# Four expert tiles instead of three with each routing head, the index lookup on VectorE alone, and three tiles ahead of the slots' transposes

## The chip, the cores and the metric

The kernel runs on one core of one Trainium2 chip. The metric is the device time of one execution in microseconds (us), as the median of several executions. TensorE is called PE below (its weight loads PEld), VectorE DVE, ScalarE ACT, GpSimd POOL and SyncE SP; L53 is line 53 of the kernel before.

## What is computed

Two layers of a streaming encoder on 512 tokens of 1024 channels, in float32: a convolution with gated linear attention, then an attention with forget gates. Each layer ends with a PEER feed-forward part, and only that part is touched by the change. Cut to what matters:

```python
PEER_HEADS = 8; PEER_NKEYS = 128; PEER_TOPK = 16        # 128*128 experts, 128 slots per token

def peer_ffn(h, wq, keys, u, v):
    q = (h @ wq).reshape(B, S, PEER_HEADS, 2, half)
    s1 = einsum('bshd,hnd->bshn', q[..., 0, :], keys[:, 0])
    s2 = einsum('bshd,hnd->bshn', q[..., 1, :], keys[:, 1])
    v1, i1 = top_k(s1, 16);  v2, i2 = top_k(s2, 16)
    cand = (v1[..., :, None] + v2[..., None, :]).reshape(B, S, PEER_HEADS, 256)
    sc, j = top_k(cand, 16)
    experts = take_along_axis(i1, j // 16) * 128 + take_along_axis(i2, j % 16)
    gates = softmax(sc)
    act = gelu(einsum('td,ted->te', h, u[experts]))
    return einsum('te,ted->td', gates * act, v[experts])
```

## The kernel before

A PEER part (`peer`, `peer_body`; once for each layer) runs in three stretches.

**Routing.** The loop over 8 heads projects the queries of a head (`proj_T` twice: 24 matmuls of 512 columns each), multiplies them with the keys (L990), copies the scores to SBUF (`sd`, L991) and calls `route`. That does, on DVE, the top 16 of each of the two key halves for four token blocks (`topk`, L740 to L745), the 64 candidate sums, and their top 16. The lookup of the indices is a closure, `lookup()`, that runs a head later: ACT casts the indices (`ix`, L773), DVE takes the differences of neighbouring ones (`dx`, L777), ACT spreads each difference over 16 places (`st`, L780), DVE compares positions with steps (`oh`, L798, twice), multiplies by the spread differences (L801) and folds the products (L805, L807) into the ids `E`. All these are bf16.

**Expert tiles.** With 128 tokens the experts' rows are gathered by indirect DMA; for the other 352 tokens all 16384 experts are computed densely, 128 at a time: 128 tiles of the matrix u. A tile (`u_step`) loads 512 KB, splits the float32 weights into a high part (ACT, `whi`, L52) and a low part (DVE, or POOL where the call says so, `wlo`, L53), and makes 24 matmuls of 352 columns into the PSUM tile `pu`; ACT takes the Gelu (`xact` or `act`, L871). `WQU` = 3 tiles are written behind each head's `route`, so 24 belong to the routing. 32 of the first tokens of the second block are gathered as well (`x_u`: a gather on POOL, then a dot product of 1024 elements on DVE, L897); up to `XR` = 2 such rows go with each head.

**The rest of the first half.** After the last head, the gates are normalised (`gates`, L820 on), PE transposes the ids and gates of the slots (`flip`, L929), and 104 more tiles follow. With them go 96 pieces of `gate4` (POOL, ACT and DVE make one-hot tiles `a1`, `a2`, PE multiplies them, L959, ACT copies the result to `big`) at an even pace from the first tile on to `TAIL` = 8 tiles before the end, and the gathers that are left with their dots (L881).

**The second half** sweeps 128 tiles of the matrix v (L1053) and gathers rows of v (L914).

The order on each engine is not the program's. The scheduler of the framework orders the instructions of the whole program by its own simulated times, and each engine then takes its row first in, first out. `issue_after` pins an instruction behind another. So the counts below are taken from the order on each engine.

## Time and profile before

| | us |
|---|---|
| median of 3 runs (lowest, highest) | 3182.42 (3172.59, 3187.05) |
| the profiled execution's own time | 3180.49 |
| its span, first to last instruction | 3178.7 |
| layer 0, first scores of the routing to the transposes | 304.7 to 540.0 |
| layer 0, transposes to the end of the first half | 540.0 to 1031 |
| layer 1, the same two stretches | 1918.0 to 2147.8 to 2640 |

The share of busy time is read by stretch: an engine that is busy for nearly all of a stretch, and that the others wait for, bounds it. In rows of the timeline the brackets hold the idle time of that engine just before the instruction and what ended it. PEclk is the clock that was granted to TensorE, as a share of 2.4 GHz.

### The profile page before, as it was taken

Reading aid. Unit: us, or ns where it says so; the run is one execution under the profiler, and the core shown is the slowest. Engines: PE = TensorE matmul, PEld = TensorE weight load, DVE = VectorE, ACT = ScalarE, POOL = GpSimd, SP = SyncE. Lnnn points to the kernel's source line nnn. Section 1 sums busy time; section 2 is a strip of 40 time slices with the busy share of each in tenths; the row PEclk is TensorE's granted clock in tenths of the full one; section 3 lists DMA queues with packets and bytes.
Section 4 is the critical chain, followed back from the end, with each engine's and each line's share of the span. In section 5 each row is a group of like instructions: output and inputs, shape, how many; then the busy total and the mean of one; then the engine's idle time right before and its main releaser. Section 6 shows DMA issues by size and latency. Waiting matters only on the chain.

```text
span 3178.7 us, 46471 instructions
## 1 busy us (share of the span) xinstructions
PE 3024.8 (95%) x15934; PEld 2635.8 (83%) x15934; DVE 2466.8 (78%) x5338; ACT 1541.1 (48%) x2668; POOL 1394.1 (44%) x1072
## 2 busy tenths in 40 slices
PE   8999996999999999999999989969999999999999
PEld 6767886999999888887766669869999997887787
DVE  7764999888787888888546538998877888888886
ACT  4353334777765333333356624337667753333333
POOL 1321233999786233333100012328999983332330
PEclk9999997999999999999999999989999999999999
DMA  4104554999999999999421125558999999999996
GB/s 154 60 27 131 178 182 137 344 368 357 338 336 337 323 355 359 346 358 346 149 80 43 39 83 178 166 181 293 340 347 330 342 340 332 369 354 336 361 346 211
DMA packets 343808, 815.00 MB, mean 256 GB/s; under 512 B 27897, under 2 KB 182922, under 8 KB 337426
## 3 DMA queue, kind: packets, MB, share of 16 engines
q1 hardware_dynamic: 260626, 510.00, 46.2%
q0 software_dynamic: 82944, 302.03, 26.8%
q8 instruction: 125, 2.05, 0.3%
q14 instruction: 113, 0.93, 0.1%
HBM read 717.74 MB, written 93.06 MB: 255 GB/s over the span
## 4 chain that ended last, share of the span: by engine, by line
PE 74%; DVE 8%; DMA 2%; ACT 1%; issue 1%; POOL 0%; SPq 0%; DVEq 0%; ACTq 0%; POOLq 0%
PE acc L1053 32%; PE pu L75 9%; PE pu L77 9%; PE pu L76 9%; PE bank L959 5%; PE bank L77 2%; PE bank L75 2%; PE bank L76 2%; PE po L672 1%; PE bank L640 1%; DVE wlo L53 1%; DVE gr L897 1%; DVE tk L743 1%; DMA raw<-in_vF_dram 1%; ACT whi L52 1%
## 5 line engine op out<-in xcount | busy, mean ns | idle before, releaser
L52 ACT ACTIVATE whi<-raw 128x1024 fp32r<-128x1024 f32 x604 | 634.7, 1056 | 643.2 <-PE pu L76 310.6
L53 DVE TENSOR_TENSOR wlo<-raw,whi 128x1024 fp32r<-128x1024 f32 x565 | 693.0, 1227 | 194.8 <-ACT whi L52 193.8
L75 PE MATMUL pu<-hhi,whi 128*128 128x352 f32 x2048 | 687.1, 335 | 13.3 <-ACT xact L871 10.2
L77 PE MATMUL pu<-hhi,wlo 128*128 128x352 f32 x2048 | 671.8, 328 | 12.9 <-DVE wlo L53 11.9
L76 PE MATMUL pu<-hlo,whi 128*128 128x352 f32 x2048 | 669.3, 327 | 0.6 <-DVE hlo L115 0.6
L914 POOL DMA_INDIRECT gr<-in_vF_dram,ids x256 | 329.6, 1287 | 664.0 <-DVE x L916 620.2
L1053 PE MATMUL acc<-wlo,wh 128*128 128x512 f32 x1536 | 474.4, 390 | 0.0
L1053 PE MATMUL acc<-whi,wl 128*128 128x512 f32 x1536 | 471.7, 389 | 0.0
L1053 PE MATMUL acc<-whi,wh 128*128 128x512 f32 x1536 | 430.7, 392 | 24.1 <-ACT wh L52 13.8
L52 ACT ACTIVATE wh<-gc 128x384 fp32r<-128x384 f32 x256 | 134.2, 525 | 644.5 <-PE acc L1053 628.0
L879 POOL DMA_INDIRECT gr<-in_uN_dram,ids x256 | 406.3, 1587 | 83.3 <-issue 37.1
L942 POOL TENSOR_SCALAR a<-cst,sT 128x128 f32<-128x128 f32 x384 | 425.7, 1118 | 38.2 <-ACT sT L930 19.3
L75 PEld LDWEIGHTS pu<-hhi,whi 128*128 128x128 f32 x2048 | 391.6, 191 | 17.8 <-ACT xact L871 12.7
L77 PEld LDWEIGHTS pu<-hhi,wlo 128*128 128x128 f32 x2048 | 390.5, 191 | 14.4 <-DVE wlo L53 13.1
L76 PEld LDWEIGHTS pu<-hlo,whi 128*128 128x128 f32 x2048 | 391.5, 191 | 1.7 <-DVE hlo L115 0.9
L1053 PEld LDWEIGHTS acc<-whi,wh 128*128 128x128 f32 x1536 | 288.7, 189 | 88.4 <-ACT whi L52 14.6
L1053 PEld LDWEIGHTS acc<-wlo,wh 128*128 128x128 f32 x1536 | 289.8, 189 | 60.3
L1053 PEld LDWEIGHTS acc<-whi,wl 128*128 128x128 f32 x1536 | 288.6, 188 | 59.9
L916 DVE SCALAR_TENSOR_TENSOR x<-gr,dots,x 128x1024 f32<-128x1024 f32 x256 | 327.4, 1279 | 0.4
L881 DVE CUSTOM_DVE_ANT_0 gr<-gr,h 128x1024 f32<-128x1024 f32 x256 | 309.5, 1230 | 15.7 <-DMA gr<-in_uN_dram,ids 14.9
L53 POOL TENSOR_TENSOR wlo<-raw,whi 128x1024 fp32r<-128x1024 f32 x39 | 101.4, 2606 | 497.6 <-ACT whi L52 497.5
L53 DVE TENSOR_TENSOR wl<-gc,wh 128x384 fp32r<-128x384 f32 x256 | 141.9, 555 | 120.9 <-ACT wh L52 118.5
(264 smaller groups left out, 4529.4 us busy)
## 6 DMA issues: line engine op xcount, KB each, us to landing
raw<-in_uT_dram SPq DMA_DIRECT2D x256, 512.0 KB
raw<-in_vF_dram SPq DMA_DIRECT2D x256, 512.0 KB
G<-big SPq DMA_DIRECT2D x48, 1024.0 KB
gc<-G SPq DMA_DIRECT2D x32, 1536.0 KB
aside<-xact SPq DMA_DIRECT2D x208, 176.0 KB
at<-aside SPq DMA_DIRECT2D x104, 352.0 KB
raw<-in_w_in_dram SPq DMA_DIRECT2D x32, 512.0 KB
raw<-in_wq_dram SPq DMA_DIRECT2D x32, 512.0 KB
```

The costliest lines, as they stand in the source:

```text
L52: first = self.nc.scalar.activation(hi, raw, AF.Copy)
L53: self.last_lo = (eng or self.nc.vector).tensor_tensor(lo, raw, hi.bitcast(F32), op=ALU.subtract)
L75: mm(out, lh, rh, start=first, stop=False)
L76: mm(out, lh, rl, start=False, stop=False)
L77: return mm(out, ll, rh, start=False, stop=last)
L879: nc.gpsimd.indirect_dma_start(out=r, out_offset=None, in_=uN, in_offset=bass.IndirectOffsetOnAxis(ap=ids[:, s:s + 1], axis=0))
L881: return lambda: nc.vector.tensor_tensor_reduce(r, r, h0, 1.0, 0.0, ALU.mult, ALU.add, accum_out=dots[:, s:s + 1])
L914: nc.gpsimd.indirect_dma_start(out=r, out_offset=None, in_=vF, in_offset=bass.IndirectOffsetOnAxis(ap=ids[:, s:s + 1], axis=0))
L916: return lambda: nc.vector.scalar_tensor_tensor(self.x0, r, dots[:, s:s + 1], self.x0, op0=ALU.mult, op1=ALU.add)
L942: nc.gpsimd.tensor_scalar(a2[:, t], self.iota, e2[:, t:t + 1], None, op0=ALU.is_equal)
L959: nc.tensor.matmul(p[:, t], a2[:, t], a1[:, t], start=True, stop=True)
L1053: nc.tensor.matmul(acc[b][c], wt[:, s], vt[:, c], start=(n == 0 and wt is wh and vt is vh), stop=(n == NE1 - 1 and wt is wl))
```

## The change

It does four things. `WQU` is 4, so 32 tiles are written with the heads and 96 behind them. The lookup is no longer a closure that runs a head later: it stands at the end of `route`, all of it on DVE, without the copies `ix` and `st` (the differences come from the integer indices, and the multiplication reads `dx` with each element repeated 16 times). `PLAIN` = 3 tiles stand ahead of the transposes and of the first piece of `gate4`; the 96 pieces are paced over the 85 tiles from there to `TAIL`. `XR` is 3 for every head.

```diff
@@ -30,7 +30,7 @@
 TX = 32
 XQ = P // TX
 TU = TD - TX
-XR = 2
+XR = 3
 TG = 16
 NTG = TD // TG
 EC = 8
@@ -38,7 +38,8 @@
 ROWS = 5
 LAG = 2
 AHEAD = 4
-WQU = 3
+WQU = 4
+PLAIN = 3
 TAIL = 8
 NEG = -3.0e38
 TILE = {"schedule_with_timeline_sim": True}
@@ -766,48 +767,39 @@
         for b in range(n):
             self.topk(sb, cand[:, b], 64, SC[:, b, hd], j[:, b])
 
-        def lookup():
-
-            ix = sb.tile([P, n, 2, 1 + TOPK], BF16, name="ix")
-            nc.gpsimd.memset(ix[:, :, :, 0:1], 0.0)
-            nc.scalar.activation(ix[:, :, :, 1:], i1, AF.Copy)
-            dx = sb.tile([P, 2, n, TOPK], BF16, name="dx")
-            ixw = ix.rearrange("p b w k -> p w b k")
-            for w in range(2):
-                nc.vector.tensor_tensor(dx[:, w], ixw[:, w, :, 1:], ixw[:, w, :, 0:TOPK], op=ALU.subtract)
-            wide = [P, 2 * n, TOPK, TOPK]
-            st = sb.tile([P, 2 * n, TOPK * TOPK], BF16, name="st", tag="rs", bufs=2)
-            nc.scalar.activation(st.rearrange("p b (r k) -> p b r k", k=TOPK),
-                                 dx.rearrange("p w b r -> p (w b) r")[:, :, :, None].to_broadcast(wide), AF.Copy)
-            jf = sb.tile([P, n, TOPK], F32, name="jf")
-            nc.vector.tensor_copy(jf, j)
-
-
-            pl = sb.tile([P, 2, n, TOPK], BF16, name="pl")
-            nc.scalar.activation(pl[:, 0], jf, AF.Copy)
-            bits = sb.tile([P, 3, n, TOPK], U32, name="bits")
-            j2 = sb.tile([P, 3, n, TOPK], F32, name="j2")
-            for k, (m, end) in enumerate(((3, 56.0), (4, 40.0), (8, 16.0))):
-                nc.vector.tensor_scalar(bits[:, k], j, m, None, op0=ALU.bitwise_and)
-                nc.vector.scalar_tensor_tensor(j2[:, k], jf, end, bits[:, k], op0=ALU.is_lt, op1=ALU.mult)
-            nc.vector.tensor_tensor(j2[:, 0], j2[:, 0], j2[:, 1], op=ALU.add)
-            nc.vector.tensor_tensor(pl[:, 1], j2[:, 0], j2[:, 2], op=ALU.add)
-
-            oh = sb.tile([P, 2 * n, TOPK * TOPK], BF16, name="oh", tag="rs", bufs=2)
-            for w in range(2):
-                nc.vector.tensor_tensor(oh[:, w * n:(w + 1) * n].rearrange("p b (r k) -> p b r k", k=TOPK),
-                                        pl[:, w, :, None, :].to_broadcast([P, n, TOPK, TOPK]),
-                                        self.steps[:, w, None].to_broadcast([P, n, TOPK, TOPK]), op=ALU.is_ge)
-            nc.vector.tensor_tensor(oh, oh, st, op=ALU.mult)
-
-            for m in (1, 2, 4):
-                pair = oh.rearrange("p b (r h m) -> p b r h m", h=2, m=m * TOPK)
-                nc.vector.tensor_tensor(pair[:, :, :, 0, 0:TOPK], pair[:, :, :, 0, 0:TOPK], pair[:, :, :, 1, 0:TOPK],
-                                        op=ALU.add)
-            nc.vector.tensor_tensor(E[:, :, :, hd].rearrange("p w b k -> p (w b) k"), oh[:, :, 0:TOPK],
-                                    oh[:, :, 8 * TOPK:9 * TOPK], op=ALU.add)
-
-        return lookup
+        dx = sb.tile([P, 2, n, TOPK], BF16, name="dx")
+        ixw = i1.rearrange("p b w k -> p w b k")
+        nc.vector.tensor_copy(dx[:, :, :, 0:1], ixw[:, :, :, 0:1])
+        nc.vector.tensor_tensor(dx[:, :, :, 1:], ixw[:, :, :, 1:], ixw[:, :, :, 0:TOPK - 1], op=ALU.subtract)
+
+
+        jf = sb.tile([P, n, TOPK], F32, name="jf")
+        nc.vector.tensor_copy(jf, j)
+        pl = sb.tile([P, 2, n, TOPK], BF16, name="pl")
+        nc.vector.tensor_copy(pl[:, 0], jf)
+        bits = sb.tile([P, 3, n, TOPK], U32, name="bits")
+        j2 = sb.tile([P, 3, n, TOPK], F32, name="j2")
+        for k, (m, end) in enumerate(((3, 56.0), (4, 40.0), (8, 16.0))):
+            nc.vector.tensor_scalar(bits[:, k], j, m, None, op0=ALU.bitwise_and)
+            nc.vector.scalar_tensor_tensor(j2[:, k], jf, end, bits[:, k], op0=ALU.is_lt, op1=ALU.mult)
+        nc.vector.tensor_tensor(j2[:, 0], j2[:, 0], j2[:, 1], op=ALU.add)
+        nc.vector.tensor_tensor(pl[:, 1], j2[:, 0], j2[:, 2], op=ALU.add)
+
+        oh = sb.tile([P, 2 * n, TOPK * TOPK], BF16, name="oh")
+        for w in range(2):
+            nc.vector.tensor_tensor(oh[:, w * n:(w + 1) * n].rearrange("p b (r k) -> p b r k", k=TOPK),
+                                    pl[:, w, :, None, :].to_broadcast([P, n, TOPK, TOPK]),
+                                    self.steps[:, w, None].to_broadcast([P, n, TOPK, TOPK]), op=ALU.is_ge)
+        ohs = oh.rearrange("p b (r k) -> p b r k", k=TOPK)
+        nc.vector.tensor_tensor(ohs, ohs, dx.rearrange("p w b r -> p (w b) r")[:, :, :, None].to_broadcast(
+            [P, 2 * n, TOPK, TOPK]), op=ALU.mult)
+
+        for m in (1, 2, 4):
+            pair = oh.rearrange("p b (r h m) -> p b r h m", h=2, m=m * TOPK)
+            nc.vector.tensor_tensor(pair[:, :, :, 0, 0:TOPK], pair[:, :, :, 0, 0:TOPK], pair[:, :, :, 1, 0:TOPK],
+                                    op=ALU.add)
+        nc.vector.tensor_tensor(E[:, :, :, hd].rearrange("p w b k -> p (w b) k"), oh[:, :, 0:TOPK],
+                                oh[:, :, 8 * TOPK:9 * TOPK], op=ALU.add)
 
     def gates(self, sb, SC):
 
@@ -965,14 +957,7 @@
 
 
         nu = 0
-        xq, rows, lookups = [], [], []
-
-        def found():
-            f, hd = lookups.pop(0)
-            f()
-            x_ids(hd)
-            xq.extend((x_u, (hd, c)) for c in range(XQ))
-
+        xq, rows = [], []
         with tc.tile_pool(name=f"pr{L}", bufs=2, reuse_waits="tile") as rb:
             for hd in range(HEADS):
                 qT = []
@@ -989,18 +974,16 @@
                     for w in range(2):
                         nc.tensor.matmul(p[:, w], qT[w][:, b * P:(b + 1) * P], kt[:, w], start=True, stop=True)
                     nc.scalar.activation(sd[:, b], p.rearrange("p a b -> p (a b)"), AF.Copy)
-                lookups.append((self.route(rb, sd, E, S, hd), hd))
+                self.route(rb, sd, E, S, hd)
+                x_ids(hd)
+                xq.extend((x_u, (hd, c)) for c in range(XQ))
                 for i in range(WQU):
                     lo, mm = u_step(nu, nc.gpsimd if nu < 2 or nu > 12 and nu % 2 else None)
                     nu += 1
-                    if i == 0 and hd:
-                        with tc.issue_after(lo.ins):
-                            found()
                 with tc.issue_after(lo.ins):
                     for f in rows:
                         f()
-                rows = pump(xq, XR if hd < HEADS - 1 else 2 * XR)
-            found()
+                rows = pump(xq, XR)
             self.gates(rb, S)
         nc.vector.tensor_scalar(idf, E[:, 0, 0].rearrange("p h k -> p (h k)"), float(NE1),
                                 float(L * NE1 * P), op0=ALU.mult, op1=ALU.add)
@@ -1008,14 +991,12 @@
 
 
         with tc.tile_pool(name=f"pu{L}", bufs=2, reuse_waits="tile") as ub:
-            for b in range(nd):
-                flip(b)
             groups = [(b, tg) for b in range(nd) for tg in range(P // TG)]
             groups = groups[TX // TG:] + groups[0:TX // TG]
             gates = [(gate4, (ub, b, tg, g)) for b, tg in groups for g in range(TG // 4)]
             gathers = xq + [(g_u, (s,)) for s in range(SLOTS)]
             nx = len(xq)
-            ng, nq = len(gates) / (NE1 - TAIL - nu), len(gathers) / (NE1 - LAG - nu)
+            ng, nq = len(gates) / (NE1 - TAIL - PLAIN - nu), len(gathers) / (NE1 - LAG - nu)
             cg = cq = 0.0
             products, rows = [], [rows] + [[] for _ in range(LAG - 1)]
             while nu < NE1:
@@ -1024,9 +1005,13 @@
                 with tc.issue_after(mm.ins):
                     for f in products:
                         f()
-                cg += ng
-                products = pump(gates, cg)
-                cg -= int(cg)
+                    if nu == HEADS * WQU + PLAIN:
+                        for b in range(nd):
+                            flip(b)
+                if nu >= HEADS * WQU + PLAIN:
+                    cg += ng
+                    products = pump(gates, cg)
+                    cg -= int(cg)
                 with tc.issue_after(lo.ins):
                     for f in rows.pop(0):
                         f()
```

Behind the last head of layer 0, ACT prepares the tiles (`whi`), takes their Gelu (`xact`) and makes the lookup's copies, up to the first copy of transposed slots (`sT`). Before:

```order
L871 ACTIVATE xact<-pu 128x352
L52 ACTIVATE whi<-raw 128x1024
L871 ACTIVATE xact<-pu 128x352
L52 ACTIVATE whi<-raw 128x1024
L773 ACTIVATE ix<-i_4292 128x8x16
L52 ACTIVATE whi<-raw 128x1024
L780 ACTIVATE st<-dx 128x2048
L787 ACTIVATE pl<-jf 128x64
L820 ACT_TABLE_LOAD
L820 ACTIVATE S<-S 128x512
L930 ACTIVATE sT_2054<-bank 128x384
```

Now:

```order
L863 ACTIVATE xact<-pu 128x352
L53 ACTIVATE whi<-raw 128x1024
L863 ACTIVATE xact<-pu 128x352
L53 ACTIVATE whi<-raw 128x1024
L863 ACTIVATE xact<-pu 128x352
L53 ACTIVATE whi<-raw 128x1024
L812 ACT_TABLE_LOAD
L812 ACTIVATE S<-S 128x512
L53 ACTIVATE whi<-raw 128x1024
L922 ACTIVATE sT_2054<-bank 128x384
```

The copies `ix`, `st` and `pl` are gone from ACT. On PE the tiles counted in each order before a layer's first transpose are 27 before and 37 now, in both layers; 101 and 91 follow it.

On DVE, the lookup of a middle head of layer 0 (`oh`, `dx`, `pl`), among the top-k of the next head and splits of tiles (`wlo`). Before:

```order
L794 TENSOR_TENSOR pl<-j_3491 128x64
L743 MATCH_REPLACE tk<-v_3364,sd 128x128 x2
L798 TENSOR_TENSOR oh<-pl,steps 128x1024
L744 MAX v_3364<-tk 128x8 x2
L53 TENSOR_TENSOR wlo<-raw,whi 128x1024
L801 TENSOR_TENSOR oh<-oh,st 128x2048
L745 MAX_INDEX i_3365<-v_3364,tk 128x8 x2
L805 TENSOR_TENSOR oh<-oh 128x64x16
```

Now:

```order
L779 CAST pl<-jf 128x64
L784 SCALAR_TENSOR_TENSOR j_3621<-jf,bits 128x64 x3
L790 TENSOR_TENSOR oh<-pl,steps 128x1024
L785 TENSOR_TENSOR j_3621<-j_3621 128x64
L786 TENSOR_TENSOR pl<-j_3621 128x64
L790 TENSOR_TENSOR oh<-pl,steps 128x1024
L741 MAX v_3874<-sd 128x8 x2
L794 TENSOR_TENSOR oh<-oh,dx 128x2048
```

One cast came over from ACT, and the multiplication takes `dx` in place of `st`. Counted from the first scores to the last write of `E` in a layer, DVE now makes 28 dots (L897) instead of 21, and 32 splits (L53) in layer 0 and 33 in layer 1 instead of 27.

On POOL, the splits and the gathers of the later heads of layer 0, up to the first one-hot tile (`a`). Before:

```order
L53 TENSOR_TENSOR wlo<-raw,whi 128x1024 x2
L772 MEMSET ix 128x8 x2
L53 TENSOR_TENSOR wlo<-raw,whi 128x1024
L895 DMA gr<-in_uN_dram,idx 128x1024 x3
L53 TENSOR_TENSOR wlo<-raw,whi 128x1024 x2
L895 DMA gr<-in_uN_dram,idx 128x1024 x2
```

Now:

```order
L54 TENSOR_TENSOR wlo<-raw,whi 128x1024 x3
L887 DMA gr<-in_uN_dram,idx 128x1024 x4
L54 TENSOR_TENSOR wlo<-raw,whi 128x1024 x2
L887 DMA gr<-in_uN_dram,idx 128x1024 x8
L871 DMA gr<-in_uN_dram,ids 128x1024
L934 TENSOR_SCALAR a_4953<-cst,sT_2054 128x128 x2
```

POOL splits three times with a later head, two tiles and one projection, where it split two or three times; over the eight heads that is 4 splits more, the odd ones of tiles 24 to 31.

## Rows read from the trace of the kernel before

**Rows 1.** The page's head: busy us of each engine, share of the span, instructions.
```profile
PE 3024.8 (95%) x15934; PEld 2635.8 (83%) x15934; DVE 2466.8 (78%) x5338; ACT 1541.1 (48%) x2668; POOL 1394.1 (44%) x1072
```

**Rows 2.** Busy us by stretch: both routings, what follows each, one second half.
```profile
core 0: us, PE busy (x) PEld busy (x) DVE busy (x) ACT busy (x) POOL busy (x), PEclk, DMA share, GB/s
304.70:540.00 235.30, 197.99 (x1046) 180.72 (x1044) 227.71 (x1053) 84.65 (x134) 65.89 (x45) 0.91 0.53 170
540.00:1031.00 491.00, 481.32 (x3202) 480.10 (x3202) 394.74 (x780) 339.69 (x683) 416.23 (x331) 0.99 0.93 337
1035.00:1560.00 525.00, 521.14 (x2288) 430.25 (x2288) 425.27 (x513) 189.83 (x256) 152.33 (x124) 1.00 0.95 333
1918.00:2147.80 229.80, 193.94 (x1057) 177.36 (x1055) 226.33 (x1053) 85.85 (x136) 62.87 (x45) 0.94 0.54 177
2147.80:2640.00 492.20, 483.80 (x3202) 482.97 (x3202) 394.34 (x780) 337.86 (x681) 441.01 (x330) 1.00 0.94 334
```

**Rows 3.** Timeline of PE (start, us): the first transposes of each layer.
```profile
540.05 0.69 PE L929 MATMUL bank<-cst,E 128*128 128x128 f32 x2 [16.08 <-DVE E L807]
...
2147.86 0.69 PE L929 MATMUL bank<-cst,E 128*128 128x128 f32 x2 [16.29 <-DVE E L807]
```

**Rows 4.** Busy us by stretch, as Rows 2: the end of layer 0's routing.
```profile
510.00:545.00 35.00, 17.27 (x71) 16.40 (x72) 31.77 (x138) 10.40 (x22) 8.85 (x11) 0.62 0.48 154
```

**Rows 5.** Groups of DVE, 330 to 510 us: count, busy us, mean ns, idle before.
```profile
L53 DVE TENSOR_TENSOR wlo<-raw,whi 128x1024 fp32r<-128x1024 f32 x20 | 24.2, 1209 | 0.0
L897 DVE CUSTOM_DVE_ANT_0 gr<-gr,hx 128x1024 f32<-128x1024 f32 x17 | 20.4, 1224 | 3.6 <-DMA gr<-in_uN_dram,idx 3.6
...
L798 DVE TENSOR_TENSOR oh<-pl,steps 128x1024 bf16<-128x1024 bf16 x12 | 13.5, 1129 | 0.1
...
L805 DVE TENSOR_TENSOR oh<-oh 128x1024 bf16<-128x1024 bf16 x6 | 8.9, 1476 | 0.0
L801 DVE TENSOR_TENSOR oh<-oh,st 128x2048 bf16<-128x2048 bf16 x6 | 7.3, 1216 | 0.0
...
L777 DVE TENSOR_TENSOR dx<-ix 128x64 bf16<-128x64 bf16 x12 | 3.8, 330 | 0.0
...
L794 DVE TENSOR_TENSOR pl<-j 128x64 bf16<-128x64 f32 x6 | 1.3, 214 | 0.1
```

**Rows 6.** Timeline of DVE: a wait for a gather, and one comparison twice.
```profile
374.75 1.23 DVE L897 CUSTOM_DVE_ANT_0 gr<-gr,hx 128x1024 f32<-128x1024 f32 x1 [2.77 <-DMA gr<-in_uN_dram,idx]
...
381.12 2.89 DVE L798 TENSOR_TENSOR oh<-pl,steps 128x1024 bf16<-128x1024 bf16 x1
...
390.94 0.68 DVE L798 TENSOR_TENSOR oh<-pl,steps 128x1024 bf16<-128x1024 bf16 x1
```

**Rows 7.** Groups of POOL, 330 to 510 us, and its timeline at 381 us.
```profile
L53 POOL TENSOR_TENSOR wlo<-raw,whi 128x1024 fp32r<-128x1024 f32 x12 | 32.3, 2699 | 72.9 <-ACT whi L52 72.9
...
380.98 2.48 POOL L53 TENSOR_TENSOR wlo<-raw,whi 128x1024 fp32r<-128x1024 f32 x1 [3.79 <-ACT whi L52]
```

**Rows 8.** Timeline of PE: products of consecutive gate pieces, layer 0 and layer 1.
```profile
643.92 1.05 PE L959 MATMUL bank<-a,a 128*128 128x128 f32 x8
644.73 0.41 PE L75 MATMUL pu<-hhi,whi 128*128 128x352 f32 x1
...
648.61 1.05 PE L959 MATMUL bank<-a,a 128*128 128x128 f32 x8
...
2344.80 1.05 PE L959 MATMUL bank<-a,a 128*128 128x128 f32 x8
2345.61 0.41 PE L75 MATMUL pu<-hhi,whi 128*128 128x352 f32 x1
...
2349.68 1.05 PE L959 MATMUL bank<-a,a 128*128 128x128 f32 x8
```

**Rows 9.** Groups of POOL, 600 to 950 us, as Rows 5.
```profile
L942 POOL TENSOR_SCALAR a<-cst,sT 128x128 f32<-128x128 f32 x145 | 165.0, 1148 | 8.7 <-ACT whi L52 6.4
L879 POOL DMA_INDIRECT gr<-in_uN_dram,ids x99 | 146.1, 1476 | 31.6 <-DVE dots L881 12.6 <-issue 12.0 <-DVE a L952 3.0
```

## Prediction

> **What bounds the kernel now.** The page's head comes first: PE is busy for 95% of the span and no other engine for over 83% [rows 1]. That is an average over stretches, so the second view is the busy time by stretch [rows 2]. In the first half's later part and in the second half PE is busy for 98 to 99% of the time. In the two routings it is not: there DVE is busy for 227.7 of 235.3 us and 226.3 of 229.8 us, PE only for 198.0 and 193.9 us. The routing ends in both layers with a hole on PE of 16 us before the transposes, and what ends it is DVE's last write of the ids [rows 3]. So DVE bounds the routing and PE the rest. The change hands PE more tiles inside the routing, where it has time, and takes them out of the part where PE is the bound. What it costs is whatever it gives to DVE before those last ids.
>
> **What PE gains.** By the order, 37 tiles lie before a layer's transposes instead of 27, so 91 follow instead of 101. A tile behind the transposes takes, from its first matmul to the next products, 3.88 us in layer 0 (644.73 to 648.61) and 4.07 us at the place shown in layer 1 (2345.61 to 2349.68) [rows 8]. Both paces occur, so I take 3.95: ten tiles are **39.5 us a layer** (38.8 to 40.7). They fit in the routing: PE has some 37 us free in each, and DVE will make the routing longer. The pieces of `gate4` and their products are as many as before (0.81 us each), only closer together: 96 over 85 tiles, 1.13 a tile instead of about one.
>
> **What DVE gets**, from the first scores to the last ids, where it has 7.6 us idle in layer 0 and 3.5 us in layer 1 [rows 2], so that nearly all of it lengthens the stretch:
> - Dots of gathered rows: 28 instead of 21, 7 of 1.224 us [rows 5] = 8.6 us.
> - Splits: 5 more in layer 0, 6 in layer 1, of 1.209 us [rows 5]: 6.7 us on average. The other new tiles' splits are POOL's.
> - The multiplication of the lookup, one per head. No row shows a bf16 multiplication with a factor repeated in its innermost dimension. The lower bound is the present one, 2048 elements in 1.216 us. The upper bound is a rate of one element per step: two splits, float32, of 1024 elements in 1.209 us each, together 2.42 us [rows 5]. L798 shows what is fixed: 1024 elements take 0.68 us [rows 6] where 2048 of L801 take 1.216, so 0.54 us is for 1024 elements and 0.14 us is fixed. The split then spends 1.07 us on its 1024 elements, half of L798's pace, and 2048 at that pace take 2.28 us. I take this, since the factor no longer runs through memory element by element: 1.06 us more, 8 times, 8.5 us (0 to 9.6).
> - One cast more (0.214 us, as L794), and in place of two differences of 0.330 us one cast of 8 elements and one difference of 120, each about as L794 [rows 5]: 8 heads of +0.21 - 0.66 + 0.43, about 0 (-2 to +2).
> - POOL's splits. There are 4 more, and they cost DVE time: a split on POOL starts at 380.98 and takes 2.48 us [rows 7], L798 begins at 381.12 and takes 2.89 us, and 0.68 us where POOL is quiet [rows 6]. Over 330 to 510 us L798's mean is 0.45 us above 0.68 (12 times, 5.4 us), L805's 0.8 us above the same 0.68 for as many elements (6 times, 4.8 us), L777's 0.12 us above L794's (12 times, 1.4 us) [rows 5]: 11.6 us for 12 splits of POOL, about 1 us each. For 4 more I take 4.6 us, since the lookup's instructions now stand closer together (0 to 8.8, at 2.2 each).
>
> The sum is 28.4 us. I take 1 us off for idle time that gets filled: **27.4 us a layer** (13 to 38). The low end is dots and splits less 2; the high end is every upper bound with one more wait for a gather such as the one of 2.77 us [rows 6]. ACT's removed copies gain nothing: ACT is busy for 85 of 235 us there [rows 2]. The deferral of the lookup is given up at no cost as long as DVE has a queue of ready work, and its order shows that the next head's top-k starts before the folds of the last.
>
> The Trainium skill ("VectorE: DVE Perf Modes", section "Mode 2×_1P — pack two bf16 into one 32-bit read") speaks against this edit: two 16-bit values per step need a step of one element in every operand, and the repeated factor has a step of zero. Its table for 2048 bf16 elements has 1224 ns at the double rate, where the trace has 1216, and 2293 ns at the single rate. By the page the term is an estimated 8.6 us, without its rule 0, and the forecast would be 17 us lower.
>
> **The join.** PE's hole before the transposes shrinks, since there is more to do in it. In the stretch around it PEclk is 0.62 [rows 4], and 0.99 over the 491 us behind it [rows 2], which is about 10 us at half speed and so 5 us lost. I count 2 us of it as won (0 to 7).
>
> **Behind the transposes** POOL gets tight. In 600 to 950 us its two groups are busy for 311 us over 72.5 pieces of two one-hots each, 4.29 us a piece: 2.30 for one-hots and 2.02 for gathers [rows 9]. At 1.13 pieces a tile and gathers at 1.447 instead of 1.41 a tile (136 over 94, 144 over 102, by the code) that is 2.59 + 2.07 = 4.66 us a tile. 12.0 us of "issue" over 99 gathers add 0.17: 4.83 us. PE needs 3.88 + 1.13 x 0.81 = 4.79 us. So POOL is level with PE. Its durations are mostly waits (a one-hot's mean of 1.15 us lies in front of DVE's long instructions), and it has waits now that are nobody's bound (12.6 us for dots). I take 3 us lost a layer (0 to 8).
>
> **Sum.** A layer gains 39.5 + 2 - 27.4 - 3 = 11 us, two layers 22 us. The profiled execution took 3180.5 us, 1.9 below the median of the three runs, so the time is **3158 us**, 0.7% less. Its own range is 3142 to 3174: 5 us a layer on the DVE sum, and the two paces of the tiles, which I can't assign.
>
> **Rivals.**
> 1. *The lookup is cheap.* The multiplication keeps its rate and POOL's splits hit top-k instructions, which show no such stretching. DVE gets 14.3 us, a layer gains 39.5 + 2 - 14.3 - 3 = 24 us: 3132 us. Against it: nothing in the rows shows the rate with a repeated factor.
> 2. *The routing eats it.* DVE's sum comes out at 38 us, by splits on POOL that each cost 2.2 us and by dots that wait for their gathers behind POOL's row of three splits (2.7 us each [rows 7]). The hole before the transposes stays as it is. A layer gains 39.5 - 38 - 3, about -1.5 us: 3184 us.
> 3. *POOL becomes the bound* behind the transposes, the case that ends slower. If its instructions stretch by 5% because DVE is denser there, a tile takes POOL 4.66 x 1.05 + 0.17 = 5.06 us against PE's 4.79, and 85 tiles lose 23 us. A layer then loses 39.5 + 2 - 27.4 - 23 = -9 us, the kernel is at 3198 us and above. It decides from the point where POOL needs over 4.79 us a tile for good; a few late pieces alone are caught up in the 8 tiles at the end. For it: the level sum above. Against it: POOL's own idle time now. The Trainium skill ("SBUF — State Buffer", section "Who interferes with whom") has the mechanism, an exclusive lock between GpSimd and DVE instructions with two SBUF inputs, in which the first comer blocks the other; the trace agrees on DVE's side [rows 6, 7].
>
> **How the numbers follow.** Forecast 0.50, rival 1 0.15, rival 2 0.22, rival 3 0.13. A measurement of this kernel can tell about 0.5% (16 us) from no change, so faster means under 3165. Two thirds of the forecast's own range lie there, which with rival 1 makes 0.49. The rest of the forecast and rival 2 make 0.38 for the same, rival 3 0.13 for slower. The range runs from rival 1's time to short of rival 3's: 3132 to 3190.
>
> **What would show it.** The two routings, first scores to transposes, should take 262 and 257 us with DVE still busy for over 96%; the stretches behind them some 453 us. The multiplication should take 2.28 us. L798's counterpart should still show durations of 2 us and more beside splits on POOL. Behind the transposes, PE should wait for nothing, and the pieces should stand 4.2 us apart on average. The prediction is wrong if PE, not DVE, ends up waited for in the routing, or if PE waits for one-hots of POOL.

## The result and the profile of the changed kernel

The changed kernel takes **3206.26 us** (3197.05 to 3213.67, 5 runs) against 3182.42 us: ratio 1.0082, 95% interval 1.0059 to 1.0104. A second set gave 1.0088 (1.0062 to 1.0114). It is slower, where 3158 us were forecast. The profiled execution took 3213.67 us (span 3211.9), the slowest of its five, so the stretches below are compared with each other and not summed to the median. PE is busy for 95% of the span as before [rows 1], and nothing else in the page's head shows the loss.

The busy time by stretch does; the columns are those of [rows 2], and the stretches are both routings (first scores to first transpose) and what follows each up to the v sweep's first matmul.

```profile
305.64:578.46 272.82, 238.28 (x1282) 219.69 (x1280) 261.44 (x1082) 80.13 (x127) 74.52 (x45) 0.94 0.53 175
578.46:1047.57 469.11, 451.35 (x2963) 447.84 (x2963) 372.97 (x754) 325.04 (x663) 392.08 (x327) 0.98 0.94 334
1937.99:2207.79 269.80, 235.54 (x1296) 216.51 (x1295) 264.45 (x1082) 82.06 (x131) 76.66 (x45) 0.96 0.53 179
2207.79:2673.61 465.82, 453.25 (x2962) 451.56 (x2962) 376.20 (x754) 324.19 (x662) 384.57 (x327) 0.99 0.95 336
```

The routings were 235.3 and 229.8 us [rows 2] and are 272.8 and 269.8: 37.5 and 40.0 us longer, where 27.4 were forecast. The stretches behind the transposes were 495.1 and 492.7 us up to the same matmul and are 469.1 and 465.8: 26.0 and 26.9 us shorter, where 38.5 were forecast. The four together are 24.6 us longer, about what the medians differ by. The two profiled spans themselves lie 33.2 us apart; most of the rest is layer 0's v sweep with the odd mixing behind it (890.4 instead of 882.9 us), which the edits hardly touch. DVE still fills the routing (261 of 273 us, 264 of 270).

The groups of DVE over 330 to 510 us, to be read against [rows 5] (the busy us depend on what falls into the window, the means and idle times do not):

```profile
L889 DVE CUSTOM_DVE_ANT_0 gr<-gr,hx 128x1024 f32<-128x1024 f32 x20 | 31.4, 1568 | 7.2 <-DMA gr<-in_uN_dram,idx 7.2
L54 DVE TENSOR_TENSOR wlo<-raw,whi 128x1024 fp32r<-128x1024 f32 x19 | 24.8, 1306 | 0.0
...
L794 DVE TENSOR_TENSOR oh<-oh,dx 128x2048 bf16<-128x2048 bf16 x5 | 11.4, 2276 | 0.0
...
L799 DVE TENSOR_TENSOR oh<-oh 128x1024 bf16<-128x1024 bf16 x6 | 9.1, 1514 | 0.0
L773 DVE TENSOR_TENSOR dx<-i 128x120 bf16<-128x120 uint32 x5 | 7.9, 1585 | 0.0
L790 DVE TENSOR_TENSOR oh<-pl,steps 128x1024 bf16<-128x1024 bf16 x10 | 6.9, 688 | 0.2
```

The multiplication (L794) is where the prediction put it, 2.28 us. The dots (L889) were 1.224 us each and are 1.568, with 7.2 us of waits for gathers instead of 3.6. The subtraction of 120 elements (L773), put at about 0.2 us, has a mean of 1.585. The comparison (L790), 1.129 before, has come down to 0.688. So the stretching has moved from one line to others. Two timelines, of DVE and of POOL, show how:

```profile
416.01 1.23 DVE L889 CUSTOM_DVE_ANT_0 gr<-gr,hx 128x1024 f32<-128x1024 f32 x1 [0.21 <-DMA gr<-in_uN_dram,idx]
...
417.17 2.46 DVE L773 TENSOR_TENSOR dx<-i 128x120 bf16<-128x120 uint32 x1
```

```profile
416.93 2.56 POOL L54 TENSOR_TENSOR wlo<-raw,whi 128x1024 fp32r<-128x1024 f32 x1
```

A split on POOL starts 0.24 us ahead of the subtraction, which then ends 0.14 us behind the split. For each DVE instruction that overlaps a split on POOL, I took its duration less that of the same instruction alone (the median of those that overlap none). This is called the stretching below. Over the routings it is 16.8 and 15.2 us before (13 splits of POOL each, 1.3 and 1.2 us for a split) and 26.8 and 28.8 us now (17 each, 1.6 and 1.7 us for a split); the second profile of the changed kernel has 25.3 and 27.6. Two expectations below were written with other figures (27.5 and 29.5 now, 20.3 and 16.9 before); the traces give these. Top-k instructions inside a split keep their length (0.28 us for a FIND_INDEX8 over 128 elements, inside and elsewhere).

Behind the transposes PE waits for POOL now, which it did not before. First what PE waited for in 578.46 to 1047.57 us and in 2207.79 to 2673.61, then POOL's timeline at layer 0's transposes:

```profile
PE bank L951 <- POOL a L934: 7.0, 6, 3.1
PE pu L76 <- ACT xact L863: 5.5, 5, 2.5
```

```profile
PE bank L951 <- POOL a L934: 3.9, 3, 1.9
```

```profile
579.61 0.94 POOL L887 DMA_INDIRECT gr<-in_uN_dram,idx  x1 [26.71 <-DVE idx L882]
580.85 0.94 POOL L887 DMA_INDIRECT gr<-in_uN_dram,idx  x1 [0.30 <-issue]
582.09 0.94 POOL L887 DMA_INDIRECT gr<-in_uN_dram,idx  x1 [0.30 <-issue]
583.34 0.94 POOL L887 DMA_INDIRECT gr<-in_uN_dram,idx  x1 [0.31 <-issue]
584.58 1.29 POOL L871 DMA_INDIRECT gr<-in_uN_dram,ids  x1 [0.30 <-issue]
585.90 5.86 POOL L934 TENSOR_SCALAR a<-cst,sT 128x128 f32<-128x128 f32 x6
```

PE's first transpose stands at 578.46. Four gathers of the last head, whose ids come with the last E, and one more stand on POOL ahead of the first one-hots, which begin 7.4 us later. In the kernel before they began at 541.58, 1.5 us after the transposes, with no gather between:

```profile
541.58 3.86 POOL L942 TENSOR_SCALAR a<-cst,sT 128x128 f32<-128x128 f32 x6 [9.63 <-ACT sT L930]
```

### The profile page after: what moved, and what is told of

It reads as the page before. It is cut to its first block, busy times and chain, and to the rows that moved or that the text cites. A ratio compares the mean times of both kernels' runs of the same rounds, so it can differ in the third digit from the quotient of the medians.

```text
span 3211.9 us, 46617 instructions
## 1 busy us (share of the span) xinstructions
PE 3052.4 (95%) x15934; PEld 2654.5 (83%) x15934; DVE 2497.7 (78%) x5346; ACT 1502.7 (47%) x2620; POOL 1363.1 (42%) x1064
## 4 chain that ended last, share of the span: by engine, by line
PE 69%; DVE 12%; issue 4%; DMA 3%; ACT 2%; POOL 1%; SPq 0%; DVEq 0%; POOLq 0%; ACTq 0%
PE acc L1038 31%; PE pu L76 7%; PE pu L77 7%; PE pu L78 7%; PE bank L951 5%; PE bank L78 3%; PE bank L76 2%; PE bank L77 2%; DVE wlo L54 2%; DVE gr L889 2%; DMA gr<-in_uN_dram,idx 2%; PE po L673 1%; PE bank L641 1%; ACT whi L53 1%; DVE oh L794 1%
## 5 line engine op out<-in xcount | busy, mean ns | idle before, releaser
L53 ACT ACTIVATE whi<-raw 128x1024 fp32r<-128x1024 f32 x604 | 633.5, 1055 | 784.0 <-PE pu L77 348.9
L54 DVE TENSOR_TENSOR wlo<-raw,whi 128x1024 fp32r<-128x1024 f32 x557 | 684.7, 1229 | 213.6 <-ACT whi L53 212.6
L78 PE MATMUL pu<-hhi,wlo 128*128 128x352 f32 x2048 | 676.5, 330 | 24.4 <-DVE wlo L54 23.4
L906 POOL DMA_INDIRECT gr<-in_vF_dram,ids x256 | 353.5, 1381 | 626.9 <-DVE x L908 577.4
L1038 PE MATMUL acc<-whi,wh 128*128 128x512 f32 x1536 | 418.6, 392 | 21.1 <-ACT whi L53 12.2
L53 ACT ACTIVATE wh<-gc 128x384 fp32r<-128x384 f32 x256 | 134.0, 525 | 626.8 <-PE acc L1038 618.2
L934 POOL TENSOR_SCALAR a<-cst,sT 128x128 f32<-128x128 f32 x384 | 398.1, 1046 | 32.6 <-PE bank L951 22.5
L871 POOL DMA_INDIRECT gr<-in_uN_dram,ids x256 | 363.2, 1419 | 111.9 <-DVE dots L873 66.4
L1038 PEld LDWEIGHTS acc<-whi,wh 128*128 128x128 f32 x1536 | 288.7, 189 | 85.8 <-ACT whi L53 16.8
L54 POOL TENSOR_TENSOR wlo<-raw,whi 128x1024 fp32r<-128x1024 f32 x47 | 122.6, 2612 | 533.6 <-ACT whi L53 533.4
L78 PE MATMUL bank<-hhi,wlo 128*128 128x512 f32 x512 | 208.7, 408 | 33.0 <-DVE wlo L54 33.0
```

The costliest lines, as they stand in the source:

```text
L53: first = self.nc.scalar.activation(hi, raw, AF.Copy)
L54: self.last_lo = (eng or self.nc.vector).tensor_tensor(lo, raw, hi.bitcast(F32), op=ALU.subtract)
L78: return mm(out, ll, rh, start=False, stop=last)
L871: nc.gpsimd.indirect_dma_start(out=r, out_offset=None, in_=uN, in_offset=bass.IndirectOffsetOnAxis(ap=ids[:, s:s + 1], axis=0))
L906: nc.gpsimd.indirect_dma_start(out=r, out_offset=None, in_=vF, in_offset=bass.IndirectOffsetOnAxis(ap=ids[:, s:s + 1], axis=0))
L934: nc.gpsimd.tensor_scalar(a2[:, t], self.iota, e2[:, t:t + 1], None, op0=ALU.is_equal)
```

## The experiments

All times are medians; ratios are to the kernel before, measured beside each (medians of 3177 to 3185 us), so kernels are compared by ratio. Routings and stretches behind the transposes come from each kernel's own profile, layer 0 and layer 1.

| kernel | us | ratio (95%) | routings | behind |
|---|---|---|---|---|
| before | 3182 | 1 | 235.3, 229.8 | 495.1, 492.7 |
| changed | 3206 | 1.0082 (1.0059-1.0104) | 272.8, 269.8 | 469.1, 465.8 |
| changed_again | 3210 | 1.0088 (1.0062-1.0114) | 269.9, 269.3 | 466.3, 472.0 |
| no_pool_splits | 3205 | 1.0068 (1.0048-1.0087) | 259.4, 262.6 | 467.4, 465.4 |
| pool_first_only | 3192 | 1.0038 (1.0020-1.0056) | 261.5, 263.5 | 465.1, 466.1 |
| old_lookup | 3199 | 1.0047 (1.0032-1.0061) | 260.7, 265.0 | 476.7, 469.3 |
| new_lookup_only | 3208 | 1.0084 (1.0058-1.0109) | 238.2, 244.0 | 488.2, 486.4 |
| new_lookup_deferred | 3193 | 1.0047 (1.0028-1.0066) | 241.8, 237.2 | 493.9, 498.1 |
| three_tiles | 3203 | 1.0073 (1.0047-1.0099) | 256.1, 255.0 | 483.3, 491.6 |
| four_tiles_in_before | 3176 | 0.9978 (0.9962-0.9994) | 249.2, 249.4 | 470.9, 473.5 |
| no_tiles_ahead | 3223 | 1.0120 (1.0100-1.0139) | 270.1, 267.0 | 468.9, 473.3 |
| two_rows | 3192 | 1.0025 (1.0010-1.0040) | 264.7, 264.2 | 456.1, 456.9 |
| rows_held | 3188 | 1.0033 (1.0017-1.0050) | 266.3, 263.3 | 456.4, 452.7 |
| pool_first_in_before | 3166 | 0.9943 (0.9925-0.9961) | 223.5, 224.4 | 490.2, 501.9 |
| three_edits_back | 3158 | 0.9929 (0.9907-0.9951) | 245.7, 246.1 | 457.1, 455.7 |
| one_row | 3165 | 0.9936 (0.9915-0.9958) | 241.5, 241.9 | 464.0, 454.0 |
| three_back_rows_held | 3138 | 0.9879 (0.9854-0.9905) | 235.7, 235.4 | 450.6, 453.5 |

**How far one profile can be trusted.** 

> The changed kernel as it is, once more, beside the other three of this set, to see what a second profile of the same program shows stretch by stretch. If the longer routings are the kernel's own (theory A), they come out at 272.8 and 269.8 us again within some 2 us, while the stretches in which TensorE bounds (behind the transposes, the v sweeps, the odd mixing) move by up to 10 us with the pace of TensorE; the median is 3206 us within 5. If the first profile was an outlier (theory B: it was the slowest of its five runs), the routings come out 10 us or more shorter.

Theory A: the routings repeat within 3 us, the stretches behind within 6.2, the v sweep of layer 0 with the odd mixing within 4 (890.4 and 886.5). Over all kernels that last stretch, which the edits hardly touch, lies between 873 and 901 us. So a routing in one profile is good to some 3 us, the rest to about 10, and totals need the repeated runs.

**Splits on POOL.** In the changed kernel:

```diff
-p = self.proj_T(A["wq"][L, 2 * hd + w], hT, nc.gpsimd if w or not hd else None)
+p = self.proj_T(A["wq"][L, 2 * hd + w], hT)
-lo, mm = u_step(nu, nc.gpsimd if nu < 2 or nu > 12 and nu % 2 else None)
+lo, mm = u_step(nu)
```

> The changed kernel, with one edit: the splits of the routing's weights (wq and the u tiles of the heads) that stood on POOL are done on VectorE, so that POOL does no split inside the routing. Theory A (a split on POOL costs VectorE more than doing it itself): in the changed kernel's trace the VectorE instructions that overlap a split on POOL are longer than their like by 27.5 us in layer 0 and 29.5 us in layer 1, for 17 splits each; the same splits on VectorE are 17 x 1.21 = 20.6 us. So each routing gets shorter by 7 to 9 us, and the kernel takes about 3190 us against 3206. No VectorE instruction of the routing should then be much longer than its like (the subtraction dx at 0.27 us each time, dots at 1.22). Theory B (POOL's splits are a help, the long instructions only take waits that would come anyway): the 20.6 us come on top, each routing is some 290 us, and the kernel takes about 3245 us.

The routings got 13.4 and 7.2 us shorter, though DVE has 16 splits more in layer 0. The subtraction dx, all 16 times (min/median/max ns):

```profile
L773 DVE TENSOR_TENSOR dx<-i x16: 266/284/323, 321.2 to 2167.2; 128x120 bf16<-128x120 uint32 x16
```

In the changed kernel the same line of its own profile reads:

```profile
L773 DVE TENSOR_TENSOR dx<-i x16: 269/1369/2474, 318.4 to 2193.3; 128x120 bf16<-128x120 uint32 x16
```

And the dots of the whole routing of layer 0 are at 1.223 us:

```profile
L889 DVE CUSTOM_DVE_ANT_0 gr<-gr,hx 128x1024 f32<-128x1024 f32 x28 | 34.2, 1223 | 7.9 <-DMA gr<-in_uN_dram,idx 7.7
```

No split on POOL is left to overlap, and what is over 0.1 us longer than its like anyway adds up to 0.5 and 0.4 us. DVE's busy time falls from 261.4 and 264.5 us to 250.5 and 252.1, with 16 splits more in each. Theory A holds in the routing: a split on POOL costs DVE more than doing it. The waits for gathers ahead of the dots stay (9.8 and 3.6 us in the changed kernel, 7.9 and 8.9 here), so splits on POOL are not their cause, which is open; in layer 1 their growth takes back part of the gain. The total can't be told from the changed kernel's by these few runs; the first scores came 3.4 us later, since splits ahead of the routing had moved too. With those kept on POOL:

```diff
+p = self.proj_T(A["wq"][L, 2 * hd + w], hT, nc.gpsimd if not hd else None)
+lo, mm = u_step(nu, nc.gpsimd if nu < 2 else None)
```

> The changed kernel with the splits on POOL kept for the first head's query weights and the first two tiles only; all others of the routing on VectorE. With no split on POOL in the routing at all, its routings were 259.4 and 262.6 us, but its first scores came 3.4 us later. Theory A (each split on POOL costs VectorE more than its own 1.21 us): the routings are about 262 us, the first scores come as early as in the changed kernel (305.6 us), the kernel is 8 us a layer faster than the changed one, 3190 us. Theory B (what the routing gives is lost behind it): the stretches behind the transposes get 8 us longer each, and the kernel stays at 3203 us or above.

Theory A: 0.45 to 0.5% less than the changed kernel, some 15 us, and nothing is given back behind the transposes. The same edit in the kernel before:

> The kernel before with the splits on POOL kept for the first head's query weights and the first two tiles only; its lookup, three tiles a head and two gathered rows stay. It shows how much of the gain of the kernel with three edits back (3158 us) is the splits' alone. Theory A: in the kernel before 12 splits of POOL in each routing make VectorE's instructions 20.3 and 16.9 us longer, and on VectorE they are 14.5 us: each routing gets 2 to 6 us shorter, the kernel takes about 3175 us, and the rest of the gain, some 17 us, is the four tiles and the three tiles ahead of the transposes. Theory B (the splits are all of it): 3160 us or less.

It gained 0.57%, some 18 us, more than A's 7 and less than B's 22. DVE's busy time in the routings fell by 5.8 and 3.3 us, within A's 2 to 6. The stretching of 16.8 and 15.2 us accounts for only a part of that: the 12 and 13 splits more take DVE 13.6 and 14.7 us from start to next start, so that 2.6 and 2.8 us of the fall have no cause shown, and a split on POOL may cost DVE more than the stretching says. DVE's idle time fell too, from 7.6 to 1.5 us and from 3.5 to 1.3 (stretch less busy, in the rows below): its waits for gathers, 3.6 and 1.0 us before, are gone, which fits that hardly a gather stands behind a split on POOL there any more, but this was not tested by itself. Behind the transposes one stretch of this profile is 5 us shorter and the other 9 us longer; the profiled execution took 3177 us, 11 over the median.

```profile
305.22:528.68 223.46, 190.29 (x1041) 174.69 (x1039) 221.97 (x1067) 84.56 (x131) 34.52 (x32) 0.92 0.55 178
1911.19:2135.55 224.36, 192.47 (x1057) 177.64 (x1056) 223.06 (x1067) 86.33 (x135) 34.78 (x32) 0.93 0.57 181
```

**The lookup.** The changed kernel with the old instructions of the lookup, not deferred (the core of the edit):

```diff
-nc.vector.tensor_tensor(ohs, ohs, dx.rearrange("p w b r -> p (w b) r")[:, :, :, None].to_broadcast(
-    [P, 2 * n, TOPK, TOPK]), op=ALU.mult)
+nc.scalar.activation(st.rearrange("p b (r k) -> p b r k", k=TOPK),
+                     dx.rearrange("p w b r -> p (w b) r")[:, :, :, None].to_broadcast(wide), AF.Copy)
+nc.vector.tensor_tensor(oh, oh, st, op=ALU.mult)
```

> The changed kernel with the lookup of the kernel before put back (ScalarE copies the indices and spreads the factors, VectorE multiplies two full bf16 tiles), but not deferred: it stays where the changed kernel has it. Theory A (the lookup costs what its own instructions take; the splits on POOL hit whatever VectorE instruction stands there): the multiplication goes from 2.28 to 1.22 us, 8 times, 8.5 us, a cast and the differences give 1 to 2 us, the stretching stays at 27 to 30 us a layer. Each routing is 9 to 11 us shorter (263 and 260 us), the kernel about 3186 us. Theory B (the stretching belongs to the new lookup, whose subtraction dx takes 2.46 us in half of its places): 8.8 us a layer more go, and the kernel takes about 3168 us. Theory C (giving up the deferral is what costs): the kernel stays at 3200 us or above, and VectorE shows idle time in front of the lookup's instructions.

Against both profiles of the changed kernel the routings are 10.7 and 4.6 us shorter on average, near theory A. The multiplication reads 1.224 us again:

```profile
L800 DVE TENSOR_TENSOR oh<-oh,st 128x2048 bf16<-128x2048 bf16 x8 | 9.8, 1224 | 0.2
```

Its stretching is 24.4 and 28.8 us, as in the changed kernel within 2.4 us, so B is not there: without the subtraction of 120 elements the splits meet others, here a dot that takes 1.22 us alone. DVE first, then POOL:

```profile
508.85 1.84 DVE L895 CUSTOM_DVE_ANT_0 gr<-gr,hx 128x1024 f32<-128x1024 f32 x1
```

```profile
507.19 2.41 POOL L54 TENSOR_TENSOR wlo<-raw,whi 128x1024 fp32r<-128x1024 f32 x1
```

DVE's busy time less the stretching is 8.5 and 8.2 us below the changed kernel's, A's figure for the multiplication; in layer 1 DVE's idle time grew by 3.4 us and hid part of it. The total came down by 0.35 to 0.4%, 11 to 13 us, less than A's 20 us; its stretches behind are the longest of the kernels with four tiles, and why is open. The other way round, in the kernel before:

> The kernel before with only the lookup changed (all on VectorE, not deferred); three tiles a head, two gathered rows a head, transposes first. Theory A (its own instructions): 9 to 11 us more in each routing (about 245 and 240 us), the kernel about 3203 us; the hole of 16 us on TensorE in front of the transposes stays or grows. Theory B (it also draws the splits of POOL): 17 us more in each routing, about 3218 us. Theory C (as the prediction had it for all but the multiplication): 8.5 us a layer, 3199 us. If the deferral alone were worth much, VectorE would show idle time in the routing, over 7.6 and 3.5 us.

The routings got 2.9 and 14.2 us longer, 8.5 on average, as much as the multiplication's own 8 x 1.06, though two more dots fall into each routing here (23 instead of 21). The total's 0.84% is more than these two show; the profiled execution, at 3190 us, is the fastest of four that reach up to 3217. With the deferral kept:

> The kernel before with the new instructions of the lookup, but still deferred behind the next head's first tile, as before. With the new lookup and no deferral the routings were 238.2 and 244.0 us (before 235.3 and 229.8) and the median 3208 us. Theory A (the lookup costs by its multiplication, the deferral is worth nothing, since VectorE has other work ready): the routings are 8 us longer than before on average, the kernel takes about 3200 to 3208 us, as without the deferral. Theory B (giving up the deferral costs): the routings are as before plus the multiplication, but the kernel is 8 us or more below the form without it, 3198 us or less.

The routings add up to 479.0 us against 482.3 without the deferral, so it is worth nothing there that one profile can show (two dots fewer in each are 2.4 us by themselves). The totals (1.0047 and 1.0084) lie apart, but their intervals still overlap, and of the two profiled executions the deferred one was the longer. Whether the deferral is worth something outside the routing stays open.

**The tiles.** Three a head in the changed kernel, `WQU = 3`:

> The changed kernel with three tiles of the first half a head again instead of four (three gathered rows a head, the new lookup and three tiles ahead of the transposes stay). Theory A (the extra tiles pay, the rest of the change costs): each routing loses 4 splits on VectorE of 1.21 and 4 on POOL that cost VectorE some 1.6 each, 11 us (262 and 259 us), and the stretch behind the transposes gets 8 tiles of 3.95 us longer, 32 us (501 and 497 us); the kernel is 21 us a layer slower, about 3248 us. Theory B (the four tiles are what made the change slow, since their splits fill VectorE): the routing gets shorter by 30 us or more and the kernel takes 3190 us or less.

Neither. The routings are 15 us shorter (A said 11), but the stretches behind only 14 to 17 and 20 to 26 us longer, not 32: in the changed kernel the eight extra tiles win about what they cost, and by the total nothing that can be told (1.0073 against 1.0082 and 1.0088). Four a head in the kernel before, `WQU = 4`:

> The kernel before with four tiles a head and nothing else. Theory A (an extra tile costs VectorE its split, or a split on POOL of the same effect, and TensorE gains it behind the transposes): the routings are 13 to 16 us longer (250 and 245 us), the stretches behind the transposes 8 x 3.95 = 32 us shorter (463 and 461 us), a layer gains 16 to 19 us, the kernel takes about 3148 us. Theory B (as between the changed kernel and its form with three tiles, which differed by 3 us in all): what is won behind the transposes goes by waits and a slower pace, and the kernel takes about 3180 us.

Between the two: the routings cost 13.8 and 19.6 us, the stretches behind win 24.2 and 19.2, and the kernel is 0.2% faster. And no tiles ahead of the transposes in the changed kernel, `PLAIN = 0` with the transposes at the routing's end:

> The changed kernel with no tiles ahead of the transposes: they stand at the routing's end, as before, and the pieces of the one-hots are spread over 88 tiles. Theory A (three tiles of TensorE fill its hole): the routings get 3.6 us shorter by three splits, TensorE's hole in front of the transposes grows to about 16 us, the stretches behind get 3 tiles longer, 12 us; a layer loses 8 us, the kernel takes about 3222 us. Theory B (the tiles ahead take away what TensorE could do while the first one-hots are made): TensorE's waits for one-hots of POOL behind the transposes, 4 to 7 us, go as well, and the kernel stays within 5 us of 3207.

The total is A's (about 0.35% above the changed kernel, by ratios whose intervals still overlap). Of the stretches only PE's hole moved the way A had it, from 4.7 and 5.8 us to 11.3 and 13.0, not to 16.

**The rows of a head.** In the changed kernel:

```diff
-XR = 3
+XR = 2
```

> The changed kernel with two gathered rows a head instead of three; all else as changed, so that 7 of 28 dots a layer move from the routing to behind the transposes. Theory A (dots in the routing are paid, since VectorE bounds there, and are free behind the transposes): 7 x 1.22 = 8.6 us, with the share of waits for gathers (9.8 us of idle time over 28 dots, 2.4 us) and of stretching some 12 us less in each routing, 261 and 258 us; behind the transposes 0 to 3 us more; the kernel takes about 3186 us. Theory B (their work returns behind the transposes, where VectorE and POOL are dense too): those stretches get 8 us or more longer and the kernel stays above 3200 us.

By DVE's count only 3 dots left each routing (1076 instructions against 1082, two a dot), not 7, and the routings are 5 to 8 us shorter. But the stretches behind are 9 to 15 us *shorter*, which neither theory had. PE's waits for one-hots of POOL are 1.2 and 0.4 us there. That pointed to the gathers ahead of the first one-hots, and to this edit of the changed kernel, three rows kept:

```diff
-rows = pump(xq, XR)
+rows = pump(xq, XR if hd < HEADS - 1 else 0)
-ng, nq = len(gates) / (NE1 - TAIL - PLAIN - nu), len(gathers) / (NE1 - LAG - nu)
+ng, nq = len(gates) / (NE1 - TAIL - PLAIN - nu), len(gathers) / (NE1 - LAG - PLAIN - nu)
-cq += nq
+cq += nq if nu > HEADS * WQU + PLAIN else 0.0
```

> The changed kernel, in which no gather is issued between the last head and the first pieces of the one-hots (none with the last head, none with the three tiles ahead); the rows held back follow behind. Three rows stay with every other head. In the changed kernel five gathers, four of which wait for the last head's ids, stand on POOL ahead of the first one-hots, which begin 7.4 us after the transposes (585.90 against 578.46). Theory A (these gathers are why the stretch behind the transposes is 469 and 466 us): the first one-hots begin within 3 us of the transposes, TensorE's waits for one-hots of POOL fall from 7.0 and 3.9 us to about 1, the stretches come near the 456 us of the form with two rows, 460 us or less; the routing keeps its 270 us; the kernel takes about 3192 us. Theory B (the waits go, but the stretch is long for another reason, such as TensorE's slower pace of 166.7 ns a matmul, half of the time in the changed kernel): the stretches are 463 us or more and the kernel takes 3200 us or more.

Theory A, by its numbers, but for the routing: with four dots fewer it did not keep its 270 us. POOL's timeline at the transposes (572.19), PE's waits in the stretch behind, and the stretches:

```profile
572.18 0.94 POOL L887 DMA_INDIRECT gr<-in_uN_dram,idx  x1 [2.12 <-DVE idx L882]
573.77 5.34 POOL L934 TENSOR_SCALAR a<-cst,sT 128x128 f32<-128x128 f32 x6 [0.65 <-ACT sT L922]
```

```profile
PE pu L76 <- ACT xact L863: 3.6, 2, 2.5
PE bank L951 <- POOL a L934: 0.9, 1, 0.9
```

```profile
305.86:572.19 266.33, 239.83 (x1280) 219.95 (x1280) 253.17 (x1079) 80.34 (x127) 79.95 (x46) 0.94 0.53 178
572.19:1028.63 456.44, 444.50 (x2965) 442.92 (x2962) 370.60 (x744) 323.65 (x662) 399.17 (x321) 0.99 0.94 338
1923.79:2187.09 263.30, 238.23 (x1296) 219.36 (x1296) 256.39 (x1079) 82.28 (x131) 77.39 (x46) 0.95 0.54 182
2187.09:2639.77 452.68, 447.81 (x2965) 446.77 (x2962) 370.55 (x747) 322.10 (x661) 388.85 (x321) 1.00 0.94 338
```

The stretches behind are 12.7 and 13.1 us shorter than in the changed kernel's first profile, more than the 6.0 and 3.6 us by which the waits for one-hots fell: without waits the products take 80.2 and 79.4 us from start to next start instead of 83.0 and 80.8, the tiles 3.2 us less in each, and the matmuls of 352 columns that start the next one 0.27 us or more later, as PE's do where it comes out of a wait, fell from 30 and 21 to 11 and 11. Part is given back: layer 1's v sweep, which now begins with eight dots of the gathers that are left instead of two, takes 549 us instead of 538. What is left is 0.5%, some 17 us. The slower pace of TensorE is not the main cause: of those matmuls that follow each other at once, 47 and 71% still run at it (46 and 78% in the changed kernel).

**Together.** Two rows, the old lookup and POOL's splits for the first weights only:

> The changed kernel with three edits together: two gathered rows a head, the lookup of the kernel before (not deferred), splits on POOL for the first head's query weights and the first two tiles only. Four tiles a head and three ahead of the transposes stay. Theory A (VectorE's work sets the routing and the three shares add up): 10 us by the splits, 8.5 by the lookup, 12 by the dots, 30 us off each routing, about 242 and 240 us; behind the transposes 468 us as in the changed kernel; the kernel takes about 3146 us, 1.2% less than before. Theory B (TensorE, busy for 238 us of the changed kernel's routing, becomes the bound): the routings stop at some 252 us, TensorE's hole in front of the transposes is gone, the kernel takes about 3166 us. Theory C (what is won in the routing is lost behind it): 3185 us or above.

3158 us, between A and B; the three single gains (some 15, 12 and 19 us by their ratios against 1.0085) add up to 46, and together they gave 50. DVE's 240 of 246 us still set the routing, so B's bound is not reached. One row instead of two:

> The kernel with three edits back (3158 us), with one gathered row a head in the routing instead of two. Theory A (dots are paid in the routing and free behind it): 7 or 8 dots fewer there, 9 us off each routing down to 237 us, where TensorE, busy for 226 us, is nearly level; behind the transposes no change; the kernel takes about 3142 us. Theory B (behind the transposes POOL and VectorE get too dense, 152 gathers over 94 tiles): those stretches get 10 us or more longer, the kernel takes 3158 us or more. Theory C: the routing gets shorter, but the v sweep starts with the rows that are left and gets longer by as much, 3155 to 3160 us.

Theory C in the main: the routings are 4 us shorter, though the eight dots that left each are 9 us by their own durations, and layer 1's v sweep takes 554 us instead of 546. Layer 0's stretch behind is 7 us longer, which is B's side. And three edits back with the rows held:

> The kernel with three edits back (3158 us) and the same holding of gathers between the last head and the first pieces. There TensorE waited for one-hots of POOL for only 0.5 us behind the transposes. Theory A (the wait is the way in which the gathers cost): nothing is left to win, the routing loses 2 to 4 dots, 2.4 to 5 us, the kernel takes 3150 to 3158 us. Theory B (they cost in another way too): the stretches behind the transposes get 5 us or more shorter than 457 and 456 us.

```profile
305.18:540.83 235.65, 226.87 (x1281) 211.06 (x1280) 229.81 (x1068) 97.06 (x151) 27.56 (x28) 0.99 0.58 186
540.83:991.44 450.61, 444.66 (x2963) 443.14 (x2963) 373.41 (x756) 324.46 (x663) 394.19 (x320) 1.00 0.94 341
1892.17:2127.52 235.35, 228.13 (x1297) 212.90 (x1296) 231.64 (x1068) 99.94 (x155) 27.89 (x28) 0.99 0.59 189
2127.52:2580.97 453.45, 444.63 (x2963) 442.88 (x2963) 377.31 (x757) 323.88 (x662) 387.62 (x323) 1.00 0.94 341
```

B holds in layer 0 (6.5 us shorter than with three edits back) and not in layer 1 (2.2). Neither theory foresaw the routings: 8 dots fewer (17 of 25 are left), 10 us each. one_row, with as few dots, takes 6 us more; why is open. With four tiles in them they now take nearly what they took before with three (235.3 and 229.8 us), the stretches behind are 39 to 45 us shorter than before, and the kernel is **1.2% faster than before** and 2.0% faster than the changed one, by their ratios.

## Why the prediction was wrong

The routing's forecast was too short by some 11 us a layer and the stretch behind too long in its gain by some 12, together some 46 us in two layers: 22 us forecast as a gain became 24 lost.

- **What bounds the kernel** was right: DVE the routing, PE the rest.
- **What PE gains.** The count was right (91 tiles instead of 101 behind the transposes). The price of 3.95 us was right for the kernel before (without waits 3.97 and 3.99 us a tile), but the tiles that are left now take 4.03 and 4.07 us: together they are 34 and 33 us shorter, not 39.5. More of their matmuls run at the slower pace (46 and 78%, before 31 and 54%), and more at the lower of the two clock levels behind PE's waits (28 and 19 that start the next one 0.29 us later, before 14 and 2). What sets the pace stays open.
- **The join**, put at 2 us won, and the 3 us lost to POOL are the steps that failed behind the transposes. With three rows a head, and gathers issued beside the three tiles ahead, no row with known ids is left at the end. So POOL begins behind the transposes with the last head's gathers, and PE waits for one-hots: 7.0 and 3.9 us, and the products take 4.3 and 2.3 us more besides. The prediction had named a wait for one-hots as a sign that it is wrong, but for another reason. rows_held, with one of these gathers left there, has stretches of 456 and 453 us; the forecast's 38.5 us off would be 457 and 454 at the same matmul.
- **What DVE gets.** Without POOL's splits the forecast's sum is 23.8 us; DVE's busy time less the stretching grew by 23.7 and 24.5, so these terms were right together. The multiplication's 8.5 us was exact (2.280 us as a mean of layer 0, 2.564 in layer 1, where a split met one). The Trainium skill ("VectorE: DVE Perf Modes", section "Mode 2×_1P — pack two bf16 into one 32-bit read") wants 16-bit values and a step of one; the trace agrees (2.28 us with the repeated factor, 1.22 without), and rival 1 fell by it.
- **POOL's splits** are the step that failed in the routing: put at 4.6 us for four more, the stretching grew by 10.0 and 13.6 us (8.5 and 12.4 in the second profile). The mean of 1 us a split was read from three lines; the DVE instructions of all lines give 1.3 and 1.2 in the kernel before, and in the new order, with more dots and the subtractions to meet, all 17 cost 1.6 and 1.7. The step also took the price as given and did not compare it with the 1.21 us that a split saves DVE. On the rows of the kernel before that would have come out about level; pool_first_in_before shows that the splits were a loss there already.
- **One us off for filled idle time** had the wrong sign: idle time grew by 3.8 and 1.9 us, and waits for gathers by 6.2 and 2.6.
- **The deferral at no cost**: held in the routing, open for the total.
- **Rivals.** Rival 2 had the routing nearly right (38 us). Its first reason, dearer splits on POOL, is borne out; its second is not: the waits for gathers grew, but no_pool_splits has them without any split on POOL, so that its number is in part luck. Rival 3's side came true by another mechanism: POOL is busy for 392 of 469 us behind the transposes, so it is not the bound; what counts is what stands ahead of its first one-hots. That the hole before the transposes shrinks (16.1 to 4.7 us, 16.3 to 5.8 [rows 3]) was forecast, and no_tiles_ahead puts the smaller hole at some 11 us in all, by ratios whose intervals overlap. Rival 2 had the hole unchanged.
